# How one sample's query and key reach 128 partitions in a retention layer: GpSimd broadcasts, or DMA through a DRAM scratch

## The chip, the core and the metric

The kernel runs on one core of a Trainium2 chip. The core has TensorE (PE, with its weight loads listed apart as PEld), VectorE (DVE), ScalarE (ACT), GpSimd (POOL) and SyncE (SP), which here issues almost all DMAs; 16 DMA engines carry them. The metric is device time in microseconds. Before the change the median of three runs is 2573.97 us (2573.81 to 2577.06).

## The reference

The program is one inference step of a two-layer trunk in float32 with width 2048: a pooling mixer, an MLP, a retention layer, a second MLP, each with a residual. It serves 272 prompt tokens (16 of them meta tokens) and 8 samples of one token, so 280 columns go through every matrix. The change lies in the retention layer, in the part that serves the samples. For each of 8 heads and each of 8 samples a state of 256 x 512 values is updated and read:

```
s_new = gamma[h] * s + outer(k, v)          # k: 256 values, v: 512 values
o     = q @ s_new                            # q: 256 values, o: 512 values
y     = head_norm(o) * silu(g);  x += y @ w_out
```

The new states are outputs too. For the prompt the same head does the chunked form (scores with decay, times values, and one final state).

## The kernel before

**Weights.** All matrices come as 388 units of 1 MB in one fixed stream, `wst`. `load_unit` (L107) loads one into a `raw` tile (three buffers), `conv_unit` (L116) splits it into a high part `wh` on ACT (L127) and a low part `wl` on DVE (L129), in two halves; for the o units of heads 5 and 6, which are in `POOLED`, the second half of `wl` is made on POOL. `mm_acc` (L142) then does three products per weight block (48 matmuls a unit, all on L147). A unit is split two units ahead of its use.

**Heads.** For each head the units are four v, two k, two q, and then a tail: four g (the gate) mixed with the four o units (output projection) of the head before. Head 0 and head 6 have only g in their tails, and head 7 has its four g, then the o units of heads 5 and 6; its own o units come last. An o unit has four PSUM tiles instead of one, each added into `xT` by DVE (L432); there are four PSUM buffers for all units.

**Attention beside the units.** `attention` (L471) is a generator: after each unit one step of it is written into the program, so that its small matmuls and the samples' work lie between the units. With `schedule_with_timeline_sim=True` a scheduler sets the final order of each engine's instructions; each engine then runs its own list strictly in order, and waits by semaphores. `keep_in_program_order` holds some DMAs in the order written.

**Samples.** State and output lie with the 512 features of v on partitions (four blocks of 128), so q and k of a sample are needed as the same row on all 128 partitions. `sample_rows` (L487) puts the columns of four samples 32 columns apart into a zeroed tile `spaced`, transposes it by four 128 x 128 transposes (L492), and ACT copies the result to `rows` (L494): now q and k of a sample are a row on one partition. It is done twice per head. In `sample` (L523) GpSimd spreads that row over all partitions:

```
bc = rp.tile([P, 2 * DK], F32, tag="bc", name="bc", bufs=2)
nc.gpsimd.partition_broadcast(bc, rows[b // 4][32 * (b % 4):32 * (b % 4) + 1, :])
```

ACT makes k times v (`kv`, L532, four pieces), DVE updates the state (L534, two halves) and reduces it against q (L537, four pieces, into `bc` itself), and the state is stored (L539). States have three buffers: sample b + 3 is loaded (L479) when the store of sample b is done. POOL has other work in the layer: the rotation of k and q (L412, L413), sums for the head norm (L586, L587), the gates (L598, L601), and the `wl` halves named above.

Of the kernel before, what the change touches and what calls it, by code (L numbers as in the profile page):

```python
# [10 lines left out]
F32 = mybir.dt.float32  # L11
# [5 lines left out]
P = 128  # L17
# [3 lines left out]
NTOK = 272  # L21
NS = 8
C = NTOK + NS
CQ = C - NMETA
H = 8
DK = 256
# [4 lines left out]
EPS = 1e-6  # L31
# [49 lines left out]
def trunk_step(ctx: ExitStack, tc: tile.TileContext, wst, xT_d, xtok_d, spool_d, xc_d, xs_d, gains_d, gB_d, band_d, cs_d,  # L81
               dec_d, kvec_d, sret_d, y_d, upt_d, ups_d, rp_d, rs_d):
    nc = tc.nc
# [17 lines left out]
    ident = pers.tile([P, P], F32, name="ident")  # L101
    e0 = pers.tile([P, 1], F32, name="e0")

    state = {"load": 0, "conv": 0, "mm": 0}
# [45 lines left out]
    def mm_tile(n):  # L150
        return pmm.tile([P, 512], F32, tag="mm", name="mm")[:, :n]

# [1 line left out]
    def prep(n, gi, cols, split=True):  # L154
        w = cols.stop - cols.start
        x = xT[:, n, cols]
# [16 lines left out]
            nc.scalar.activation(out=x, in_=x, func=AF.Copy, scale=g)  # L173

    def rsqrt(a, s):
        """a ** -0.5 into the last of s, refined by one Newton step."""
        r, t, o = s
        nc.scalar.activation(out=r, in_=a, func=AF.Sqrt)
        nc.vector.reciprocal(r, r)
        nc.vector.tensor_tensor(out=t, in0=r, in1=r, op=ALU.mult)  # L180
        nc.vector.tensor_tensor(out=t, in0=t, in1=a, op=ALU.mult)
        nc.vector.scalar_tensor_tensor(out=t, in0=t, scalar=-3.0, in1=r, op0=ALU.add, op1=ALU.mult)
        nc.vector.tensor_scalar_mul(o, t, -0.5)

    def token_rstd(parts, w, mean):
        """1 / sqrt(mean + EPS) of each token (tokens on partitions), spread on a diagonal."""
        nj = 4 if w == C else 3
        nt = w // nj
        ps = pst.tile([P, 512], F32, tag="st", name="st")
        for j in range(nj):  # L190
            for i, a in enumerate(parts):
                nc.tensor.matmul(ps[:nt, j:j + 1], a[:, j * nt:(j + 1) * nt], mean, start=(i == 0),  # L192
                                 stop=(i == len(parts) - 1))
        s = tmp.tile([P, 4, 4], F32, tag="rs", name="rs")
        a, r, t, o = [s[:nt, i, :nj] for i in range(4)]
        nc.vector.tensor_scalar_add(a, ps[:nt, :nj], EPS)
        rsqrt(a, (r, t, o))
        dg = tmp.tile([P, C], F32, tag="dg", name="dg", bufs=1)
        dg3 = dg[:nt, :w].rearrange("p (j t) -> p j t", j=nj)
        nc.vector.tensor_tensor(out=dg3, in0=ident[:nt, :nt].unsqueeze(1).to_broadcast([nt, nj, nt]),  # L200
                                in1=o.unsqueeze(2).to_broadcast([nt, nj, nt]), op=ALU.mult)
        return dg[:nt, :w]
# [13 lines left out]
    ALL = slice(0, C)  # L216
    QC = slice(NMETA, C)

    # ================= pooling mixer =================
    with tc.tile_pool(name="pp", bufs=1) as pp, tc.tile_pool(name="pd", bufs=1) as pd:  # L220
        hw = D // 2
        xTf = xT.rearrange("p a b -> p (a b)")
# [20 lines left out]
        for j, (x, r, c0, c1) in enumerate(((xc, NC, 241, 272), (xa, P, 0, 128), (xb, P, 128, 241))):  # L243
            s = st[:r, j]
# [3 lines left out]
                                           scale=1.0, scalar=0.0, accum_out=s[:, 1:2])  # L248
# [22 lines left out]
        for f in range(KT):  # L271
            w = f // 4
            fs = slice(f * P, (f + 1) * P)
            ps = patt.tile([P, 512], F32, tag="att", name="dps")[:, :C]
# [4 lines left out]
            else:  # L279
                nc.tensor.matmul(ps[:, 241:272], xc[:NC, fs], band[:NC, w, 241:272], start=True, stop=True)  # L280
                nc.tensor.matmul(ps[:, 272:280], xs[:, (f - 12) * P:(f - 11) * P], band[:, w, 280:288], start=True,
                                 stop=True)
            g = gains[:, 0, f:f + 1]
# [7 lines left out]
        for g in range(4):  # L291
            parts = begin_unit("pool")
            for i in range(4):
                n = g * 4 + i
                ps = mm_tile(C)
# [4 lines left out]
        nc.sync.dma_start(out=ups_d[:, 14], in_=xc[:NS])  # L300
        nc.gpsimd.dma_start(out=upt_d, in_=u2[NC - 15:NC])

    # ================= squared-ReLU MLP =================
    def mlp(i, cols, next_gi, split):
        T = cols.stop - cols.start
        with tc.tile_pool(name=f"mlp{i}", bufs=1) as mp:
# [40 lines left out]

    mlp(0, ALL, 2, True)

    # ================= retention =================  # L350
    with tc.tile_pool(name="rp", bufs=1) as rp, tc.tile_pool(name="rs", bufs=3) as rsp:
        cs = rp.tile([P, 2, C], F32, name="cs")
        nc.sync.dma_start(out=cs, in_=cs_d)
        kvec = rp.tile([P, H, 3], F32, name="kvec")
        nc.sync.dma_start(out=kvec, in_=kvec_d)
        mean_m = rp.tile([P, P], F32, name="mean_m")
        nc.vector.memset(mean_m, 1.0 / DV)
        spaced = rp.tile([P, 4, P], F32, name="spaced")
        nc.gpsimd.memset(spaced, 0.0)
        rtok = rp.tile([P, 3], F32, name="rtok")  # L360
        cos, sin = cs[:, 0], cs[:, 1]

        def tail_copies(src, n):
            """The prompt's last 16 columns of src [P, n, .], six times over."""
            t = rp.tile([P, 4, 6, 16], F32, tag="tail", name="tail")[:, :n]
            nc.scalar.copy(out=t, in_=src[:, :, JT[2][0]:NTOK].unsqueeze(2).to_broadcast([P, n, 6, 16]))
            return t.rearrange("p n r t -> p n (r t)")
# [68 lines left out]
        def att_ps():  # L436
            return patt.tile([P, 512], F32, tag="att", name="att")

        # values: token-major, split for the state and centred over the head's features for the output
        def v_tokens(h, j):  # L440
            vT = cur["v"]
            if j == 0:
# [17 lines left out]
            nc.scalar.activation(out=vc[:nt, j], in_=vc[:nt, j], func=AF.Identity, bias=acc[:nt, 3 + j:4 + j])  # L460

        def split(hi, lo, ps, nr, scale, r0):
            """High and low part of ps * scale; of the stacked tail rows, rows r0 to r0 + 32 of hi take the low part."""
            rows = slice(0, nr)
            nc.scalar.activation(out=hi[rows], in_=ps[rows], func=AF.Copy, scale=scale)
            if nr < P:
                rows, lo = slice(r0, r0 + 32), hi
            nc.vector.scalar_tensor_tensor(out=lo[rows], in0=ps[rows], scalar=scale[rows],
                                           in1=hi[rows].bitcast(F32), op0=ALU.mult, op1=ALU.subtract)

        def attention(h, last):  # L471
            qT, kT, vs, (vh, vl, vc) = cur["q"], cur["k"], cur["vs"], cur["vtok"]
            dec = rp.tile([P, DC], F32, tag="dec", name=f"dec{h}")
            nc.sync.dma_start(out=dec, in_=dec_d[h])
            sts = {}

            def load_state(b):
                t = rsp.tile([P, 4, DK], F32, tag="sret", name=f"s{h}_{b}")
                tc.keep_in_program_order(nc.sync.dma_start(out=t, in_=sret_d[h, b]))  # L479
                sts[b] = t  # L480

            for b in range(3):
                load_state(b)
            # queries and keys of four samples as rows on partitions 0, 32, 64 and 96
            rows = []

            def sample_rows(g):  # L487
                nc.vector.tensor_copy(spaced[:, 0:2, 0:P:32], qT[:, :, CQ - NS + 4 * g:CQ - NS + 4 * g + 4])
                nc.vector.tensor_scalar_mul(spaced[:, 2:4, 0:P:32], kT[:, :, NTOK + 4 * g:NTOK + 4 * g + 4], 1.0 / 16)
                ps = att_ps()  # L490
                for i in range(4):
                    nc.tensor.transpose(ps[:, i * P:(i + 1) * P], spaced[:, i], ident)  # L492
                r = rp.tile([P, 2 * DK], F32, tag="rows", name="rows")
                nc.scalar.copy(out=r, in_=ps)  # L494
                rows.append(r)

            sample_rows(0)
            # keys: token-major, decayed to the end of the prompt
            kdh, kdl = [rp.tile([P, n, DK], F32R, tag=f"kd{n}", name=f"kd{n}_{h}") for n in (3, 2)]
            cols = token_cols(kT, 2)  # L500
            for j in range(3):
                if j != 1:
                    ps = att_ps()
# [2 lines left out]
                    nc.tensor.transpose(ps[:RT[j], off + i * P:off + (i + 1) * P], cols(i, j), ident)  # L506
                split(kdh[:, j], kdl[:, min(j, 1)], ps[:, off:off + DK], RT[j], kvec[:RT[j], h, j:j + 1], 32)
            yield True
            # scores
            ps = att_ps()  # L510
            pr = rp.tile([P, DC], F32, tag="pr", name="pr")
            off = 0
            for j, (t0, nt, q0, nq) in enumerate(JT):
                for i in range(2):
                    nc.tensor.matmul(ps[:nt, off:off + nq], kT[:, i, t0:t0 + nt], qT[:, i, q0:q0 + nq], start=(i == 0),
                                     stop=(i == 1))
# [6 lines left out]
            def sample(b):  # L523
                if b + 3 < NS:
                    load_state(b + 3)
                bc = rp.tile([P, 2 * DK], F32, tag="bc", name="bc", bufs=2)
                nc.gpsimd.partition_broadcast(bc, rows[b // 4][32 * (b % 4):32 * (b % 4) + 1, :])  # L527
                s = sts[b]
                for z in range(2):
                    kv = rp.tile([P, 2, DK], F32, tag="kv", name="kv", bufs=2)  # L530
                    for i in range(2):
                        nc.scalar.activation(out=kv[:, i, :], in_=bc[:, 256:512], func=AF.Copy,  # L532
                                             scale=vs[:, 2 * z + i, b:b + 1])
                    nc.vector.scalar_tensor_tensor(out=s[:, 2 * z:2 * z + 2], in0=s[:, 2 * z:2 * z + 2],  # L534
                                                   scalar=GAMMA[h], in1=kv, op0=ALU.mult, op1=ALU.add)
                for i in range(4):
                    nc.vector.tensor_tensor_reduce(out=bc[:, 256:512], in0=s[:, i, :], in1=bc[:, 0:256], op0=ALU.mult,  # L537
                                                   op1=ALU.add, scale=1.0, scalar=0.0, accum_out=OS[:, i, b:b + 1])
                nc.sync.dma_start(out=rs_d[h, b], in_=s)  # L539
# [26 lines left out]
                work = {1: (prompt_o, 0), 2: (prompt_o, 1), 3: (prompt_state, 0), 4: (prompt_state, 1)}  # L566
            for b in range(NS):
                sample(b)
                if b == 3:
                    sample_rows(1)  # L570
                if b in work:
                    f, a = work[b]
                    f(a)
                yield not (last and b == 0)
            # head norm
            ps = pst.tile([P, 512], F32, tag="st", name="om")
            om = rp.tile([P, NS], F32, tag="om", name="om")
            nc.vector.tensor_reduce(out=om, in_=OS.rearrange("p v b -> p b v"), op=ALU.add, axis=mybir.AxisListType.X)  # L578
# [176 lines left out]
```

## Time and profile before

| | |
|---|---|
| median of three runs | 2573.97 us |
| the profiled execution, first to last instruction (its span) | 2567.0 us |
| lying around the span (median less span) | 7.0 us |
| PE busy in the span | 2493.4 us (97%) |
| DVE, ACT, POOL busy | 59%, 45%, 18% |
| granted TensorE clock, mean | 0.981 of full speed |
| DMA | 493.07 MB, 192 GB/s mean |

The profile is read from the wait backwards. A row of waits names who waited, who released it last, how long and how often. "issue" as releaser says that the profile shows nothing that the engine waited for. A busy PE is not a PE at full speed: its clock is granted (1.0 is 2.4 GHz, 0.5 is 1.2 GHz), so the number of matmuls in a stretch must be read beside the busy time. In a timeline, starts count; ends of matmuls overlap the next.

### The profile page before, as it was taken

What the parts mean: (1) busy time and instruction counts of PE and PEld (TensorE: products, weight loads), DVE (VectorE), ACT (ScalarE), POOL (GpSimd) and SP (SyncE); (2) the same over time, 40 slices, a digit from 0 to 9 for tenths busy, and PEclk for the clock granted to TensorE, in tenths of its full rate; (3) what the DMA queues carried; (4) which work ended last, traced back from release to release, by engine and by line L of the source; (5) the groups of instructions that cost most, each with busy time, mean ns of one, the idle gap of its engine ahead of it and who ended that gap; (6) DMA issues with size and microseconds to landing.
All of it is one profiled execution on the core that took longest, in us unless ns stands there. A gap on an engine that the chain in (4) does not pass through costs nothing. (4 is left out here: it accounts for less than half of the span.)

```text
span 2567.0 us, 46873 instructions
## 1 busy us (share of the span) xinstructions
PE 2493.4 (97%) x19590; PEld 2470.3 (96%) x19590; DVE 1526.7 (59%) x2430; ACT 1158.3 (45%) x1660; POOL 466.3 (18%) x381
## 2 busy tenths in 40 slices
PE   8999999999999999999999999868999999999997
PEld 8999999999999998999999999857999999999997
DVE  7554554554555576777867767645654554554554
ACT  5433333343344465566655656524433333433443
POOL 4210210110122112112121122214210210210222
PEclk9999999999999998999999999978999999999999
DMA  6444454454444574766757566534555554554453
GB/s 235 167 171 174 179 177 168 166 179 165 172 171 169 196 257 179 277 217 231 265 204 286 201 253 242 190 131 156 175 186 182 181 181 181 181 181 181 181 181 116
DMA packets 81943, 493.07 MB, mean 192 GB/s; under 512 B 9216, under 2 KB 12288, under 8 KB 31608
## 3 DMA queue, kind: packets, MB, share of 16 engines
q1 hardware_dynamic: 81699, 489.95, 53.4%
q8 instruction: 153, 2.51, 0.4%
q14 instruction: 59, 0.48, 0.1%
q0 software_dynamic: 32, 0.12, 0.0%
HBM read 449.94 MB, written 41.02 MB: 191 GB/s over the span
## 5 line engine op out<-in xcount | busy, mean ns | idle before, releaser
L127 ACT CAST wh<-raw 128x1024 fp32r<-128x1024 f32 x776 | 799.8, 1050 | 1181.2 <-PE mm L147 644.3
L129 DVE TENSOR_TENSOR wl<-raw,wh 128x1024 fp32r<-128x1024 f32 x768 | 998.1, 1330 | 79.4 <-ACT wh L127 78.1
L147 PE MATMUL mm<-xh,wh 128*128 128x280 f32 (+1 forms) x3584 | 492.4, 290 | 2.4 <-DVE om L578 1.2
L147 PE MATMUL mm<-xh,wl 128*128 128x280 f32 (+1 forms) x3584 | 487.0, 288 | 0.0
L147 PE MATMUL mm<-xl,wh 128*128 128x280 f32 (+1 forms) x3584 | 484.8, 287 | 0.0
L147 PEld LDWEIGHTS mm<-xh,wh 128*128 128x128 f32 x3584 | 464.4, 189 | 5.3 <-ACT wh L127 2.7
L147 PEld LDWEIGHTS mm<-xh,wl 128*128 128x128 f32 x3584 | 463.1, 188 | 0.3
L147 PEld LDWEIGHTS mm<-xl,wh 128*128 128x128 f32 x3584 | 461.9, 188 | 0.0
L318 POOL TENSOR_TENSOR hf<-r 128x280 f32<-128x280 f32 (+1 forms) x128 | 185.2, 1448 | 1156.1 <-DVE r L314 1156.1
L344 DVE TENSOR_TENSOR xT<-mm,xT 128x280 f32<-128x280 f32 (+1 forms) x128 | 56.5, 441 | 400.9 <-PE mm L147 400.9
L147 PE MATMUL mm<-hh,wh 128*128 128x280 f32 (+1 forms) x2048 | 276.3, 287 | 0.0
L147 PE MATMUL mm<-hh,wl 128*128 128x280 f32 (+1 forms) x2048 | 276.2, 287 | 0.0
L147 PE MATMUL mm<-hl,wh 128*128 128x280 f32 (+1 forms) x2048 | 276.2, 287 | 0.0
L147 PEld LDWEIGHTS mm<-hh,wh 128*128 128x128 f32 x2048 | 263.8, 188 | 0.0
L147 PEld LDWEIGHTS mm<-hh,wl 128*128 128x128 f32 x2048 | 263.8, 188 | 0.0
L147 PEld LDWEIGHTS mm<-hl,wh 128*128 128x128 f32 x2048 | 263.7, 188 | 0.0
L314 DVE SCALAR_TENSOR_TENSOR r<-mm,rstd 128x280 f32<-128x280 f32 (+1 forms) x128 | 56.3, 441 | 303.3 <-PE mm L147 303.2
L532 ACT ACTIVATE kv<-bc,vs 128x256 f32<-128x256 f32 x256 | 110.3, 499 | 96.4 <-POOL bc L527 92.3
L147 PE MATMUL mm<-yh,wh 128*128 128x264 f32 x512 | 91.8, 303 | 40.4 <-DVE xT L432 28.9
L534 DVE SCALAR_TENSOR_TENSOR s<-s,kv 128x512 f32<-128x512 f32 x128 | 88.4, 697 | 70.5 <-ACT kv L532 65.8
L527 POOL PARTITION_BROADCAST bc<-rows x64 | 59.4, 960 | 333.8 <-DVE os L537 136.0
L147 PEld LDWEIGHTS mm<-yh,wh 128*128 128x128 f32 x512 | 76.9, 202 | 43.3 <-DVE xT L432 11.6
(173 smaller groups left out, 1685.3 us busy)
## 6 DMA issues: line engine op xcount, KB each, us to landing
raw<-in_wst SPq DMA_DIRECT2D x388, 1024.0 KB, 4.8
s<-in_sret SPq DMA_DIRECT2D x64, 512.0 KB, 6.1
out_rs<-s SPq DMA_DIRECT2D x64, 512.0 KB, 5.3
out_rp<-so SPq DMA_DIRECT2D x16, 256.0 KB, 2.8
xT<-in_xT SPq DMA_DIRECT2D x4, 560.0 KB, 15.1
dec<-in_dec SPq DMA_DIRECT2D x8, 208.0 KB, 2.8
out_y<-xT SPq DMA_DIRECT2D x2, 528.0 KB
xa<-in_xtok SPq DMA_DIRECT2D x1, 1024.0 KB, 7.3
```

What stands on the lines that cost most here:

```text
L127: nc.scalar.copy(out=wh, in_=src)
L129: eng.tensor_tensor(out=wl, in0=src, in1=wh.bitcast(F32), op=ALU.subtract)
L147: nc.tensor.matmul(ps, parts[s][z][:, kk, :], rhs[k][:, cols], start=(rhs is rhs_h and z + k == 0), stop=(rhs is rhs_l and k == n - 1))
L314: nc.vector.scalar_tensor_tensor(out=r[:, :T], in0=ps, scalar=0.0, in1=rstd[:, cols], op0=ALU.max, op1=ALU.mult)
L318: nc.gpsimd.tensor_tensor(out=hf[:, :T], in0=r[:, :T], in1=r[:, :T], op=ALU.mult)
L344: nc.vector.tensor_tensor(out=xT[:, n, cols], in0=ps, in1=xT[:, n, cols], op=ALU.add)
L527: nc.gpsimd.partition_broadcast(bc, rows[b // 4][32 * (b % 4):32 * (b % 4) + 1, :])
L532: nc.scalar.activation(out=kv[:, i, :], in_=bc[:, 256:512], func=AF.Copy, scale=vs[:, 2 * z + i, b:b + 1])
L534: nc.vector.scalar_tensor_tensor(out=s[:, 2 * z:2 * z + 2], in0=s[:, 2 * z:2 * z + 2], scalar=GAMMA[h], in1=kv, op0=ALU.mult, op1=ALU.add)
```

## The change

It touches the attention of the retention layer only. Per head, the queries and keys of all eight samples are copied together into one tile `qk` (128 x 32), one plain matmul with the identity turns it into 32 rows of 128, ACT copies these to SBUF, and one DMA writes them to a scratch `rd` in DRAM. Each sample's row of 512 values is then read back by one DMA with a step of 0 over partitions, which fills all 128 partitions of `bc`. The `bc` tile now has three buffers in the pool of the states, and its load is issued right behind the load of the same sample's state. The states of the first three samples are issued after the write of the scratch. `spaced`, `sample_rows` and all `partition_broadcast` are gone.

```diff
+    with tc.tile_pool(name="rp", bufs=1) as rp, tc.tile_pool(name="rs", bufs=3) as rsp, \
+            tc.tile_pool(name="rd", bufs=2, space=bass.MemoryType.DRAM) as rdp:
...
-        spaced = rp.tile([P, 4, P], F32, name="spaced")
-        nc.gpsimd.memset(spaced, 0.0)
...
             dec = rp.tile([P, DC], F32, tag="dec", name=f"dec{h}")
             nc.sync.dma_start(out=dec, in_=dec_d[h])
-            sts = {}
+            rd = rdp.tile([NS, 4, P], F32, tag="rd", name=f"rd{h}")
+            qk = rp.tile([P, 2, 2, NS], F32, tag="qk", name="qk")
+            nc.vector.tensor_copy(qk[:, 0], qT[:, :, CQ - NS:CQ])
+            nc.vector.tensor_scalar_mul(qk[:, 1], kT[:, :, NTOK:C], 1.0 / 16)
+            ps = att_ps()
+            nc.tensor.matmul(ps[:4 * NS, 0:P], qk.rearrange("p t i b -> p (t i b)"), ident, start=True, stop=True)
+            rows = rp.tile([4 * NS, P], F32, tag="rows", name="rows")
+            nc.scalar.copy(out=rows, in_=ps[:4 * NS, 0:P])
+            tc.keep_in_program_order(nc.sync.dma_start(out=rd.rearrange("b j f -> j b f"), in_=rows))
+            sts, bcs = {}, {}
 
             def load_state(b):
                 t = rsp.tile([P, 4, DK], F32, tag="sret", name=f"s{h}_{b}")
                 tc.keep_in_program_order(nc.sync.dma_start(out=t, in_=sret_d[h, b]))
                 sts[b] = t
+                t = rsp.tile([P, 2 * DK], F32, tag="bc", name=f"bc{h}_{b}")
+                row = rd[b:b + 1].rearrange("b j f -> b (j f)")
+                tc.keep_in_program_order(nc.sync.dma_start(out=t, in_=row.to_broadcast([P, 2 * DK])))
+                bcs[b] = t
 
             for b in range(3):
                 load_state(b)
-            rows = []
-            def sample_rows(g):
...
-            sample_rows(0)
...
             def sample(b):
                 if b + 3 < NS:
                     load_state(b + 3)
-                bc = rp.tile([P, 2 * DK], F32, tag="bc", name="bc", bufs=2)
-                nc.gpsimd.partition_broadcast(bc, rows[b // 4][32 * (b % 4):32 * (b % 4) + 1, :])
-                s = sts[b]
+                s, bc = sts[b], bcs[b]
...
                 sample(b)
-                if b == 3:
-                    sample_rows(1)
```

The scheduler's order changes with it. On POOL, in the tail of head 7, this stood before (`bc` is the broadcast of a sample, `oc` the gate's product, `wl` the low half of a weight unit; an ISA row without operands is an instruction of POOL's own between two kinds of work):

```order
L601 ISA
L601 TENSOR_TENSOR oc_17212<-oc_17212,ro 128x264 x4
L527 ISA
L527 ISA bc<-rows 128x512
L129 ISA
L129 TENSOR_TENSOR wl_1_18384<-raw_18097,wh_1_18383 128x1024
```

In the same place of the changed kernel (L412 rotates q, L596 is the gate's product) POOL has:

```order
L412 TENSOR_TENSOR qT_17923<-qT_17923,rpb 128x264
L596 TENSOR_TENSOR oc_17164<-oc_17164,ro 128x264 x4
L129 TENSOR_TENSOR wl_1_18327<-raw_18034,wh_1_18326 128x1024
L129 TENSOR_TENSOR wl_1_18413<-raw_18137,wh_1_18412 128x1024
L129 TENSOR_TENSOR wl_1_18496<-raw_18244,wh_1_18495 128x1024
L129 TENSOR_TENSOR wl_1_18575<-raw_18330,wh_1_18574 128x1024
L129 TENSOR_TENSOR wl_1_18654<-raw_18416,wh_1_18653 128x1024
```

Before, the last four rows come four times more, with other `wl` halves, until sample 7's broadcast is done. Now the broadcasts and all ISA rows between kinds are gone, and the `wl` halves stand one behind the other.

On SP, around the first samples of head 7 (`s` is a state, its first number the sample; `raw` a weight unit; `out_rs` a stored state), before:

```order
L479 DMA s_2_18157<-in_sret 128x1024
L113 DMA raw_17747<-in_wst 128x2048
L113 DMA raw_17852<-in_wst 128x2048
L113 DMA raw_17935<-in_wst 128x2048
L113 DMA raw_18011<-in_wst 128x2048
L113 DMA raw_18097<-in_wst 128x2048
L113 DMA raw_18194<-in_wst 128x2048
L539 DMA out_rs<-s_0_18153 128x1024
L539 DMA out_rs<-s_1_18155 128x1024
L479 DMA s_3_18259<-in_sret 128x1024
L113 DMA raw_18301<-in_wst 128x2048
L539 DMA out_rs<-s_2_18157 128x1024
```

and in the changed kernel (`rd` is the write of the scratch, `bc` the read of a sample's row):

```order
L113 DMA raw_18034<-in_wst 128x2048
L483 DMA rd_18090<-rows 4x8x128
L488 DMA s_0_18099<-in_sret 128x1024
L492 DMA bc_0_18101<-rd_18090 128x512
L488 DMA s_1_18103<-in_sret 128x1024
L492 DMA bc_1_18105<-rd_18090 128x512
L488 DMA s_2_18107<-in_sret 128x1024
L492 DMA bc_2_18109<-rd_18090 128x512
L113 DMA raw_18137<-in_wst 128x2048
L536 DMA out_rs<-s_0_18099 128x1024
L113 DMA raw_18244<-in_wst 128x2048
L536 DMA out_rs<-s_1_18103 128x1024
```

Before, the states of samples 0 to 2 are loaded six weight units ahead of the first store; now they stand directly ahead of it, behind the write of the scratch, each followed by its row.

On DVE, in head 4, this ends with the decayed scores `pr`, which the next small matmuls of PE read (L534 a state update, L537 a reduce, `kd` keys for the prompt's state); the two updates of sample 0 stand some rows ahead of these, before:

```order
L534 SCALAR_TENSOR_TENSOR s_1_14492<-s_1_14492,kv 128x512
L432 TENSOR_TENSOR xT<-mm,xT 128x264
L534 SCALAR_TENSOR_TENSOR s_1_14492<-s_1_14492,kv 128x512
L468 SCALAR_TENSOR_TENSOR kd_4_14506<-att,kvec,kd_4_14505 128x256
L537 ISA bc,os<-s_0_14490,bc 128x256
L537 ISA os 128x1
L518 TENSOR_TENSOR pr<-att,dec_14488 128x400
L519 TENSOR_TENSOR pr<-att,dec_14488 16x16
```

and in the changed kernel, with sample 0's updates among the rows (L531 is the state update, L534 the reduce, L517 and L518 make `pr`):

```order
L531 SCALAR_TENSOR_TENSOR s_0_14463<-s_0_14463,kv 128x512
L431 TENSOR_TENSOR xT<-mm,xT 128x264
L531 SCALAR_TENSOR_TENSOR s_0_14463<-s_0_14463,kv 128x512
L534 ISA bc_0_14465,os<-s_0_14463,bc_0_14465 128x256
L534 ISA os 128x1
L467 SCALAR_TENSOR_TENSOR kd_4_14476<-att,kvec,kd_4_14475 128x256
L517 TENSOR_TENSOR pr<-att,dec_14452 128x400
L518 TENSOR_TENSOR pr<-att,dec_14452 16x16
```

In both, work that PE reads later (`xT` sums, `wl`, `pr`) stands behind the first state update of sample 0; `pr` now comes after sample 0's updates instead of after sample 1's.

## Rows read from the trace of the kernel before

**Rows 1.** The page: span; each engine's busy us, share, instructions.
```profile
span 2567.0 us, 46873 instructions
...
PE 2493.4 (97%) x19590; PEld 2470.3 (96%) x19590; DVE 1526.7 (59%) x2430; ACT 1158.3 (45%) x1660; POOL 466.3 (18%) x381
```

**Rows 2.** Stretches: length; busy us (instructions) by engine; PEclk, DMA, GB/s.
```profile
980.07:1103.73 123.66, 116.83 (x865) 112.26 (x865) 85.53 (x182) 68.29 (x113) 30.71 (x33) 0.94 0.58 210
1103.73:1212.87 109.14, 109.14 (x856) 107.25 (x856) 81.10 (x170) 64.51 (x105) 21.50 (x22) 1.00 0.67 239
...
1643.28:1780.20 136.92, 92.41 (x606) 88.33 (x604) 63.48 (x151) 47.45 (x80) 37.80 (x28) 0.78 0.39 144
```

**Rows 3.** Waits of PE, 1640 to 1790 us: us, times, longest.
```profile
PE mm L147 <- DVE xT L432: 28.5, 3, 10.7
PE mm L147 <- DVE gs L422: 7.5, 1, 7.5
PE att L547 <- DVE pr L519: 6.8, 1, 6.8
```

**Rows 4.** Waits of all engines, 1640 to 1760 us.
```profile
ACT kv L532 <- POOL bc L527: 62.9, 6, 16.5
...
POOL bc L527 <- issue: 42.4, 5, 9.4
```

**Rows 5.** Timeline of POOL, head 7: start, us, instruction [idle before <- releaser].
```profile
1726.44 0.80 POOL L527 PARTITION_BROADCAST bc<-rows  x1 [9.36 <-issue]
1734.25 2.35 POOL L129 TENSOR_TENSOR wl<-raw,wh 128x1024 fp32r<-128x1024 f32 x1 [7.01 <-issue]
```

**Rows 6.** Line 527: op xcount: ns min/median/max, first, last start.
```profile
L527 POOL PARTITION_BROADCAST bc<-rows x64: 798/803/1917, 915.5 to 1745.5; - x64
...
L527 POOLq MODIFY_POOL_CONFIG  x28: 1/6/16, 909.8 to 1736.8; - x28
```

**Rows 7.** Timeline of PE in head 4, undisturbed: start, us, instruction.
```profile
1346.17 1.71 PE L515 MATMUL att<-qT,kT 128*128 128x256 f32 x12
1347.81 2.21 PE L147 MATMUL mm<-xh,wh 128*128 128x264 f32 x16
...
1353.73 2.36 PE L547 MATMUL att<-pr,vc 128*128 128x256 f32 x12
1356.02 0.76 PE L147 MATMUL mm<-yh,wh 128*128 128x264 f32 x4
...
1361.96 2.35 PE L547 MATMUL att<-pr,vc 128*128 128x256 f32 x12
...
1370.16 0.60 PE L492 MATMUL att<-ident,spaced 128*128 128x128 f32 x4
1370.52 0.72 PE L557 MATMUL att<-vh,kd 128*128 128x512 f32 x2
...
1372.24 0.65 PE L147 MATMUL mm<-yh,wh 128*128 128x264 f32 x4
```

**Rows 8.** Timeline of ACT in head 4, around the first broadcast.
```profile
1340.37 0.58 ACT L494 COPY rows<-att 128x512 f32<-128x512 f32 x1
...
1343.30 0.90 ACT L532 ACTIVATE kv<-bc,vs 128x256 f32<-128x256 f32 x2
```

**Rows 9.** The page: DMA issues: count, KB each, median us from issue to landing.
```profile
s<-in_sret SPq DMA_DIRECT2D x64, 512.0 KB, 6.1
out_rs<-s SPq DMA_DIRECT2D x64, 512.0 KB, 5.3
out_rp<-so SPq DMA_DIRECT2D x16, 256.0 KB, 2.8
```

**Rows 10.** DMA queue, 1342 to 1396 us: packets, MB, share.
```profile
q1 hardware_dynamic: 3496, 15.16, 78.8%
```

**Rows 11.** The page: state update on DVE: count | busy us, mean ns.
```profile
L534 DVE SCALAR_TENSOR_TENSOR s<-s,kv 128x512 f32<-128x512 f32 x128 | 88.4, 697 | 70.5 <-ACT kv L532 65.8
```

**Rows 12.** Reduce on DVE, tile bc: ns min/median/max.
```profile
L537 DVE CUSTOM_DVE_ANT_0 bc<-s,bc x256: 406/418/964, 918.9 to 1752.1; 128x256 f32<-128x256 f32 x128
```

More of the change, by code (lines that the diff above doesn't have):

```diff
@@ L348, in trunk_step @@
     mlp(0, ALL, 2, True)
-    with tc.tile_pool(name="rp", bufs=1) as rp, tc.tile_pool(name="rs", bufs=3) as rsp:
+    with tc.tile_pool(name="rp", bufs=1) as rp, tc.tile_pool(name="rs", bufs=3) as rsp, \
+            tc.tile_pool(name="rd", bufs=2, space=bass.MemoryType.DRAM) as rdp:
         cs = rp.tile([P, 2, C], F32, name="cs")
@@ L480, in load_state @@
                 sts[b] = t
+                t = rsp.tile([P, 2 * DK], F32, tag="bc", name=f"bc{h}_{b}")
+                row = rd[b:b + 1].rearrange("b j f -> b (j f)")
+                tc.keep_in_program_order(nc.sync.dma_start(out=t, in_=row.to_broadcast([P, 2 * DK])))
+                bcs[b] = t
             for b in range(3):
                 load_state(b)
-            rows = []
-            def sample_rows(g):
[L488 to L495, printed above, removed]
-            sample_rows(0)
             kdh, kdl = [rp.tile([P, n, DK], F32R, tag=f"kd{n}", name=f"kd{n}_{h}") for n in (3, 2)]
```

## The prediction

> **What bounds the kernel now.** The page first: PE is busy for 2493.4 of 2567.0 us [rows 1], so on the whole only PE's own work, or one of its few gaps, can move the time. POOL, which the change relieves, is busy for 18%, and it would be wrong to stop there. The gaps are found by stretches. I cut the retention layer at the first rotation of k in each head. The four heads 2 to 5 take 109.14 us each at a granted clock of 1.00 and PE never idles (one of the four stands in the rows). Head 1 has the same units and takes 123.66 us at 0.94. From the first transpose for the samples of head 7 to its own o units 136.92 us pass at 0.78 with 606 matmuls, where an undisturbed head does 856 in 109.14 [rows 2].
>
> Next, who PE waits for in head 7: DVE, with 28.5 us for xT sums, 7.5 for a gate product and 6.8 for the scores `pr` [rows 3]. But DVE has nothing heavy there. It stands in order behind state updates, and these wait for ACT's `kv`, which waited for POOL's broadcast, 62.9 us in six waits; POOL's broadcasts began after 42.4 us of "issue" [rows 4], time in which it waited for nothing that the profile shows. The timeline of POOL gives the cause: whenever it changes between a broadcast and a `wl` half it idles, 9.36 us ahead of a broadcast of 0.80, then 7.01 ahead of a `wl` half [rows 5]. 28 MODIFY_POOL_CONFIG stand on POOL's queue at the broadcast's line [rows 6]; each broadcast that follows other work pays such a gap, and in head 7 the two kinds alternate five times. In heads 2 to 5 POOL changes kind early and the gap falls where nobody waits.
>
> **What the change removes.** *Head 7.* POOL has one kind of work left, so the alternation goes. What PE's work there takes at full clock and without a wait is read from head 4 [rows 7]. A g unit takes 1353.73 - 1347.81 = 5.92 us and an o unit 1361.96 - 1356.02 = 5.94. In the stretch lie three g and eight o units: 11 x 5.93 = 65.2. The scores take 1347.81 - 1346.17 = 1.64, two groups of L547 at 2.29 take 4.6, two groups for the prompt's state at 1372.24 - 1370.52 = 1.72 take 3.4, the two groups of transposes at 0.36 take 0.7, and the sixteen or so small matmuls that remain, at the 0.09 of a transpose, some 1.5 by estimate. Sum 77.0; the loss is 136.9 - 77.0 = 59.9 us. About 44 of it is idle (136.92 less 92.41 busy); the rest is the granted clock, 0.78 in the mean, that follows the idle time, and it comes back with it.
>
> *Head 1.* 123.66 - 109.14 = 14.5 us, the same cause: in head 1 POOL must go from broadcasts to the gates' products of head 0 and back.
>
> *Transposes.* Two groups of four at 0.36 are 0.72 us a head on PE, which is the bound. In their place stands one plain matmul of 128 columns in float32. The trace has none of this shape. L515 does 832 columns of plain float32 in 1.64 us, so 128 cost 0.25; the least is a transpose, 0.09, the most all 0.72 again. I take 0.25, the row with the same kind of matmul: 0.47 saved a head, 3.8 in eight. The Trainium skill says in "TensorE: Matmul & The Clock Gate", section "Terms", that a transpose mode makes float32 four times as fast, which speaks against trading transposes for a plain matmul. By that the new one would cost 4 x 0.09 = 0.36 and the change would save 2.9 instead of 3.8, a time of 2501; the rows give a factor of 2.8, and they decide.
>
> *Off the path.* POOL loses 64 x 0.80 = 51 us of work and ACT one of two copies of 0.58 per head [rows 6, 8]; neither engine is waited for once the gaps are gone, so this is worth nothing.
>
> **What it adds.** 64 reads of 256 KB and 8 small writes, all issued by SP. In head 4 the old copy of the rows ends at 1340.95 and ACT's first `kv` begins at 1343.30 [rows 8], 2.35 us later. Now a write to the scratch must land, then a read. The trace has neither. Per DMA the nearest row is `out_rp`, 256 KB in 128 rows like the read: 2.8 us; the far rows are a state's store and load, 5.3 and 6.1 [rows 9]. So the first row is there after 5.6 us, or at the worst after 11.4. State 0, now issued right behind the write, lands 6.1 after it, when the first half of `kv` is made. I take 5.6, because the same shape moves as in `out_rp`. Then `kv` begins at 1346.6, its first half takes 0.90, and on DVE two updates at 0.70, one reduce at 0.42 [rows 11, 12] and four smaller instructions come to some 3.5 us: `pr` is ready at 1351.0. PE asks for it at 1353.73 [rows 7]; the delay is hidden with 2.7 us to spare. At the worst `pr` comes at 1356.8, and PE waits 3.0 us in each head. Behind the waiting update stand xT sums and `wl` halves as well; these are due later than `pr`. On SP, a weight unit stands behind the reads of samples 0 to 2. SP is held by the scratch write for 2.8 to 5.3 us, while the weights have three buffers, 17.8 us of PE's work: hidden. I charge 4 us in all, 0.5 a head, for landings above the median.
>
> The DMA engines have the room: in the sample stretch of head 4 they are busy for 78.8% of 54 us with 15.16 MB [rows 10], 356 GB/s while busy, so eight reads, 2.1 MB, take 5.9 us of the 11.4 that are free.
>
> **The sum.** The profiled span is 2567.0 us; the median of the runs shown is 2573.97, so 7.0 us lie around the span, and I leave these as they are. 2574.0 - 59.9 - 14.5 - 3.8 = 2495.8 is the floor; plus 4 it is 2500 us.
>
> **Rivals.**
> *DVE becomes the bound of head 7.* Its work there, 63.48 us [rows 2], would have to fit into 77.0 us, a share of 82%; the undisturbed heads show 81.10 of 109.14, 74%. For it: PE's tiles of an o unit come free only through DVE. Against it: a share of 74% never made PE wait. If 74% is what an in-order DVE can do, head 7 takes 63.48 / 0.743 = 85.4 us, 8.4 more than the floor: 2508 with the 4.
>
> *The two chained DMAs are slow.* If write and read together take over 8.3 us (5.6 and the 2.7 to spare), `pr` is late in every head. For it: landings of states of 5.3 and 6.1 under the same load. Against it: 16 KB and 256 KB are less than 512. At 11.4 us it costs 8 x 3.0 = 24: 2520.
>
> *The DMA engines fill up, and the kernel gets slower.* In each head eight reads of one DRAM row join a stretch that is already 78.8% busy. If a read costs the engines its whole landing of 2.8 us instead of 0.74, eight take 22.4 us, 11.0 more than is free; states and weights come later by that, PE has no slack of that size, and over eight heads it is 88 us: 2495.8 + 88 = 2584, slower than before. It decides from (11.4 + 78.2 / 8) / 8 = 2.65 us a read. For it: every read takes its 128 copies from the same 2 KB. Against it: the price of bytes in the same stretch.
>
> *The change doesn't do what it says.* POOL's idle time before `wl` halves is also called "issue"; if it isn't the change of kind that causes it, head 7 stays as it is and only the transposes gain: 2570, which is no change. Against it: 28 configurations stand in the trace at the broadcast's line [rows 6], and the changed order of POOL has none between its `wl` halves.
>
> **How the numbers follow.** The forecast, 2495 to 2506, has 0.58. DVE as the bound (2506 to 2512) has 0.12, the slow chain (2512 to 2535) 0.16, a remainder between 2535 and 2568 has 0.04, no effect 0.03, slower 0.07. Faster by over 0.2% (5.1 us, about what can be told from no change) is 0.58 + 0.12 + 0.16 + 0.04 = 0.90; within 0.2% 0.03; slower 0.07. The range goes from 2491, as the small matmuls in the 77.0 are an estimate, to 2535, and leaves out 0.14.
>
> **What would show it.** Right: no MODIFY_POOL_CONFIG between `wl` halves, head 7's stretch near 77 us and head 1 near 109, both at a clock of 1.00; heads 2 to 5 at about 108.7; the new matmul near 0.25; `rd` and `bc` landing within 2.8 us each. Wrong: PE waiting for `pr` in each head (slow chain), for xT in head 7 with a busy DVE (DVE bound), or heads 2 to 5 longer than 109.1 with DMA shares near 1 (engines full). A stretch of head 7 still above 100 us would overturn the reading of POOL's gaps.

## The result, and the profile after

The changed kernel takes 2500.51 us (median of 4 runs, 2498.72 to 2501.81) where the kernel before took 2573.89 beside it (4 runs): a ratio of 0.972, 95% interval 0.970 to 0.973. The profiled execution spans 2498.0 us and took 2499.76; its line numbers are those of the changed file.

The first lines of its page answer to [rows 1]; busy us, share of the span, instructions.

```profile
span 2498.0 us, 46727 instructions
...
PE 2470.1 (99%) x19542; PEld 2447.3 (98%) x19542; DVE 1519.3 (61%) x2414; ACT 1153.0 (46%) x1652; POOL 413.4 (17%) x316
```

PE is busy for 23 us less and idle for 46 us less. The stretches of [rows 2], cut at the same instructions: head 1, head 2, and head 7 from the samples' matmul to its own o units (length; busy us of PE, PEld, DVE, ACT and POOL; PEclk, DMA share, GB/s).

```profile
979.05:1091.57 112.52, 110.54 (x859) 107.45 (x859) 83.28 (x180) 67.56 (x112) 24.26 (x25) 1.00 0.69 250
1091.57:1200.34 108.77, 108.77 (x850) 106.56 (x850) 79.12 (x168) 63.80 (x104) 14.14 (x14) 1.00 0.72 259
1629.07:1711.43 82.36, 78.00 (x599) 74.77 (x598) 70.53 (x149) 47.19 (x79) 36.61 (x20) 1.00 0.79 284
```

Head 7 gives 136.92 - 82.36 = 54.6 us, head 1 11.1, and the six other heads 2.6 together (0.37 to 0.47 each); 0.7 lies elsewhere. That is 69.0, the whole difference of the two profiled spans; the medians differ by 73.4, since the profiled execution of the kernel before was one of its shorter ones. The granted clock in head 7 is back from 0.78 to 1.00. The waits of PE there, against the 43 us in [rows 3]:

```profile
PE mm L147 <- DVE xT L431: 3.9, 3, 2.0
```

No MODIFY_POOL_CONFIG is left on any line of the retention layer. The kernel before had 28 on the broadcasts' line [rows 6] and 28 more on the lines of the work that followed broadcasts (L129 and L586 10 each, L412 and L601 4 each). What became slower is the DMAs. From the page, in the columns of [rows 9]: count, KB each, median us to landing.

```profile
s<-in_sret SPq DMA_DIRECT2D x64, 512.0 KB, 6.3
out_rs<-s SPq DMA_DIRECT2D x64, 512.0 KB, 7.2
bc<-rd SPq DMA_DIRECT2D x64, 256.0 KB, 7.6
out_rp<-so SPq DMA_DIRECT2D x16, 256.0 KB, 7.4
```

The read of a row lands after 7.6 us in the median, not after 2.8, and `out_rp`, from which I took the 2.8, now needs 7.4 itself. But only 18 of the 64 reads have a recorded landing, and none of these is of samples 0 to 2, while the prediction's step is about sample 0. For the first read of head 4, SP's issues (first fence) and ACT's timeline (second) answer to [rows 8].

```profile
1327.64 0.60 SPq L483 DMA_DIRECT2D rd<-rows  x1
...
1329.60 0.33 SPq L492 DMA_DIRECT2D bc<-rd  x1
```

```profile
1327.36 0.25 ACT L482 COPY rows<-att 32x128 f32<-32x128 f32 x1
...
1334.40 1.71 ACT L529 ACTIVATE kv<-bc,vs 128x256 f32<-128x256 f32 x4 [3.05 <-DMA bc<-rd]
```

The first `kv` begins 6.8 us behind the copy, where I had 5.6: 2.0 us from the issue of the write to that of the read, and then at most 4.8 to the landing of the read. PE does not wait for `pr` in any head.

### The profile page after: what moved, and what is told of

Same layout as the page of the kernel before. It is cut to its first block, busy times and chain, and to the rows that moved or that the text cites. A ratio compares the mean times of both kernels' runs of the same rounds, so it can differ in the third digit from the quotient of the medians.

```text
span 2498.0 us, 46727 instructions
## 1 busy us (share of the span) xinstructions
PE 2470.1 (99%) x19542; PEld 2447.3 (98%) x19542; DVE 1519.3 (61%) x2414; ACT 1153.0 (46%) x1652; POOL 413.4 (17%) x316
## 4 chain that ended last, share of the span: by engine, by line
PE 94%; DVE 2%; POOL 1%; DMA 1%; ACT 1%; issue 1%; SPq 0%; DVEq 0%; POOLq 0%; ACTq 0%
PE mm L147 90%; PE att L544 1%; PE att L554 1%; DMA u<-in_gB 1%; DVE wl L129 0%; PE att L514 0%; DVE bc L534 0%; POOL oc L593 0%; PE att L455 0%; DVE s L531 0%; DVE xl L170 0%; DVE xT L431 0%; PE st L192 0%; DMA bc<-rd 0%; PE att L505 0%
## 5 line engine op out<-in xcount | busy, mean ns | idle before, releaser
L129 DVE TENSOR_TENSOR wl<-raw,wh 128x1024 fp32r<-128x1024 f32 x768 | 987.4, 1318 | 80.4 <-ACT wh L127 79.2
L534 DVE CUSTOM_DVE_ANT_0 bc<-s,bc 128x256 f32<-128x256 f32 x256 | 109.5, 440 | 1.7
L531 DVE SCALAR_TENSOR_TENSOR s<-s,kv 128x512 f32<-128x512 f32 x128 | 92.3, 729 | 23.3 <-ACT kv L529 22.6
L166 POOL TENSOR_TENSOR ssq<-ssq,sq 128x280 f32<-128x280 f32 (+1 forms) x56 | 70.9, 1266 | 172.7 <-ACT sq L164 172.2
L147 PE MATMUL mm<-yh,wh 128*128 128x264 f32 x512 | 86.0, 288 | 6.6 <-DVE xT L431 4.4
## 6 DMA issues: line engine op xcount, KB each, us to landing
xT<-in_xT SPq DMA_DIRECT2D x4, 560.0 KB, 15.2
```

The source lines that it names most:

```text
L129: eng.tensor_tensor(out=wl, in0=src, in1=wh.bitcast(F32), op=ALU.subtract)
L147: nc.tensor.matmul(ps, parts[s][z][:, kk, :], rhs[k][:, cols], start=(rhs is rhs_h and z + k == 0), stop=(rhs is rhs_l and k == n - 1))
L166: nc.gpsimd.tensor_tensor(out=ssq[:, cols], in0=ssq[:, cols], in1=sq[:, :w], op=ALU.add)
```

## The experiments

**The theory** is that of the prediction: each change of POOL between a broadcast and other work costs 7 to 9 us on POOL, and this made the losses of head 7 and head 1. The rivals: the transposes and the new order gained the time, or the broadcast as the carrier of the data did. Head 7 is timed as above in all of them.

**e1: the kernel before, without POOL's other work in head 7.**

```diff
-POOLED = frozenset(u for u, (k, h, _) in enumerate(ORDER)
-                   if (k, h) in {("o", H - 2), ("o", H - 3)})
+POOLED = frozenset()
```

> The kernel before, with its broadcasts on POOL, but all wl halves on DVE. My theory (POOL's change between kinds of work, 7 to 9.4 us each way, is what head 7 lost): of the ten changes in head 7 two round trips are left, so most of the 59.9 us goes; head 7 from 136.9 to 80 to 100 us, the whole 2514 to 2537 us; head 1 stays at 123.7. Rival (the gain came from the new order, the transposes or the data path): head 7 stays above 120 us and the whole above 2555.

2520.06 us (2519.33 to 2520.87), ratio to before 0.979 [0.978, 0.981]: nearly three quarters of the gain without any of the change's own edits. Head 1 stayed at 123.94; head 7's stretch and PE's only wait in it:

```profile
1643.91:1733.31 89.40, 81.48 (x606) 78.59 (x604) 69.88 (x160) 48.25 (x81) 21.63 (x20) 0.92 0.62 220
```

```profile
PE att L547 <- DVE pr L519: 7.5, 1, 7.5
```

So neither the transposes nor the data path made most of head 7's loss. But this run also takes the halves off POOL. The next puts the changes of kind back and leaves all else.

**e3: the changed kernel with broadcasts that nobody reads.**

```diff
                 nc.sync.dma_start(out=rs_d[h, b], in_=s)
+                un = rp.tile([P, 1], F32, tag="un", name="un")
+                nc.gpsimd.partition_broadcast(un, OS[0:1, 3, b:b + 1])
```

> The changed kernel, and per sample one more broadcast on POOL, of one element, whose result nobody reads; the data still come by DMA. If the change of kind on POOL is the cause, seven round trips of 7 + 8.5 us stand between the wl halves of head 7 (24 us): head 7 takes 110 to 140 us and the whole 2528 to 2570. Rival (the broadcast's data and its waits were the cause): no change, 2499 to 2505. On the time around the span: 7 us if it belongs to the presence of broadcasts, 1.8 us if it was chance.

2599.64 us (2598.13 to 2602.98), ratio 1.010 [1.009, 1.012]: slower than the kernel before. POOL's timeline in head 7:

```profile
1709.37 0.81 POOL L538 PARTITION_BROADCAST un<-os  x1 [9.70 <-issue]
1717.34 2.33 POOL L129 TENSOR_TENSOR wl<-raw,wh 128x1024 fp32r<-128x1024 f32 x1 [7.17 <-issue]
1728.77 0.30 POOL L538 PARTITION_BROADCAST un<-os  x1 [9.10 <-issue]
1736.17 2.33 POOL L129 TENSOR_TENSOR wl<-raw,wh 128x1024 fp32r<-128x1024 f32 x1 [7.10 <-issue]
```

A broadcast of one element that has no reader costs the gap of [rows 5] on either side. It reads what a reduce on DVE wrote and could have made POOL wait for that, but the idle time in these rows is "issue". PE's waits in head 7, and its length:

```profile
PE mm L147 <- POOL wl L129: 59.0, 6, 14.5
PE st L192 <- POOL osq L584: 13.4, 1, 13.4
```

```profile
1647.29:1811.36 164.07, 91.17 (x600) 87.22 (x599) 62.81 (x149) 47.36 (x79) 36.74 (x28) 0.77 0.42 142
```

This shows the cause for head 7. It does not test head 1: there POOL's broadcasts for the head's samples come only behind the gates' products, and the head takes what it takes in the changed kernel:

```profile
979.27:1091.79 112.52, 110.55 (x859) 107.46 (x859) 83.21 (x180) 67.35 (x112) 27.36 (x33) 1.00 0.70 250
```

That the same gaps made the 123.66 us of head 1 is read from the kernel before and not shown by a run. There the gates' products stood behind a broadcast, and PE's longest wait in the head (2.85 us for `yh`, until 1014.39) hung on them:

```profile
1004.16 1.48 POOL L527 PARTITION_BROADCAST bc<-rows  x2 [7.79 <-issue]
1013.16 3.23 POOL L601 TENSOR_TENSOR oc<-oc,ro 128x264 f32<-128x264 f32 x4 [7.52 <-issue]
```

My size for e3 was 30 us too small: I counted POOL's own time, not the halves and the last norm behind it, nor the 4 us that heads 2 to 5 each lost (112.7 to 114.4). The time around the span was 1.7 to 1.8 us in these runs, so broadcasts do not make it.

**e2: the changed kernel, all halves on DVE.** Head 7 still lay 5.4 us over the forecast, and DVE had gone from 63.48 to 70.53 us of busy time with fewer instructions. Its timeline (first fence) beside POOL's (second):

```profile
1664.12 0.68 DVE L531 SCALAR_TENSOR_TENSOR s<-s,kv 128x512 f32<-128x512 f32 x1
1664.72 2.62 DVE L534 CUSTOM_DVE_ANT_0 bc<-s,bc 128x256 f32<-128x256 f32 x1
...
1668.56 2.58 DVE L534 CUSTOM_DVE_ANT_0 bc<-s,bc 128x256 f32<-128x256 f32 x1
```

```profile
1664.46 2.59 POOL L129 TENSOR_TENSOR wl<-raw,wh 128x1024 fp32r<-128x1024 f32 x1 [5.54 <-ACT wh L127]
1667.95 2.90 POOL L129 TENSOR_TENSOR wl<-raw,wh 128x1024 fp32r<-128x1024 f32 x1 [0.90 <-ACT wh L127]
```

A reduce that takes 0.42 [rows 12] takes 2.6 when a half on POOL has begun just before it, and it ends 0.3 us behind that half. The edit is that of e1, made in the changed kernel.

> The changed kernel with all wl halves on DVE. Theory on what is left in head 7 (82.4 us against 77): DVE's instructions of 0.42 us stretch to 2.5 while POOL makes a half, so without these head 7 takes 77 to 79 us and the whole 2495 to 2497. Rival (DVE has too much work there): eight more halves at 1.13 us are 9 us more on DVE, head 7 takes 85 to 90 us and the whole 2504 to 2508.

2500.62 us (2497.16 to 2501.63): no gain. By the same two groups of head 7 in the changed kernel (first) and here (second; count | busy us, mean ns | idle before) the stretching is gone, and the added halves cost DVE a little less than it did (the sums stand in the last section):

```profile
L534 DVE CUSTOM_DVE_ANT_0 bc<-s,bc 128x256 f32<-128x256 f32 x32 | 19.4, 614 | 0.2
...
L531 DVE SCALAR_TENSOR_TENSOR s<-s,kv 128x512 f32<-128x512 f32 x16 | 16.5, 1052 | 2.1 <-ACT kv L529 2.1
```

```profile
L534 DVE CUSTOM_DVE_ANT_0 bc<-s,bc 128x256 f32<-128x256 f32 x32 | 13.0, 415 | 0.1
L531 DVE SCALAR_TENSOR_TENSOR s<-s,kv 128x512 f32<-128x512 f32 x16 | 10.9, 683 | 2.4 <-ACT kv L529 2.2
```

The stretch and the wait that took over:

```profile
1632.19:1712.38 80.19, 76.84 (x599) 74.34 (x598) 69.69 (x160) 48.27 (x80) 12.46 (x12) 0.99 0.81 292
```

```profile
PE mm L147 <- ACT yh L597: 3.4, 1, 3.4
```

PE ran its 76.84 us of other work without a gap, then waited for head 7's own norm, which POOL made in 7.0 us beside the gates. So head 7 gained 2.2 us. The profiled execution as a whole gained nothing: its head 1 took 115.56, and after the wait for the norm the clock was at 0.50 from 1711.0 to 1717.8.

**e4: one transpose for the identity matmul.**

```diff
-            nc.tensor.matmul(ps[:4 * NS, 0:P], qk.rearrange("p t i b -> p (t i b)"), ident, start=True, stop=True)
+            nc.tensor.transpose(ps[:4 * NS, 0:P], qk.rearrange("p t i b -> p (t i b)"), ident)
```

> The changed kernel with its identity matmul (0.34 us) made a transpose, one per head. By the row of a transpose, 0.09 us, 0.25 us less per head, 2.0 in all: 2498.5. Rival (one transpose of 32 columns of weights costs the same, or the gap is hidden by something else): 2500.5.

2501.67 us (2497.16 to 2504.07), no difference that the totals can tell. The heads can tell it: 2 to 5 take 108.36 or 108.37 us each, against 108.74 or 108.77 (head 4 of the changed kernel, then of this one):

```profile
1309.08:1417.85 108.77, 108.77 (x850) 106.56 (x850) 79.16 (x168) 63.91 (x104) 14.13 (x14) 1.00 0.72 259
```

```profile
1310.58:1418.95 108.37, 108.37 (x849) 106.48 (x849) 79.27 (x168) 63.61 (x104) 14.14 (x14) 1.00 0.72 260
```

So 0.4 us a head, where I had 0.25. In the profiled execution head 1 (115.58) and head 7 (83.91) took it back.

**What head 1 does.** PE waits once in the changed kernel's head 1, 1.78 us for `yh` at 1002.75, and the same wait stands in e2 to e6 and in the second run of the changed kernel (e10). The stretch 1000 to 1010 us in the first run and in e10:

```profile
1000.00:1010.00 10.00, 8.22 (x50) 6.72 (x49) 6.57 (x17) 6.47 (x17) 3.23 (x4) 1.00 0.91 290
```

```profile
1000.00:1010.00 10.00, 8.22 (x35) 6.39 (x34) 6.89 (x17) 6.59 (x17) 3.23 (x4) 0.71 0.86 267
```

After the same gap the clock stays at 2.4 GHz in one execution and falls to 1.2 for part of the stretch in another; head 1 then takes 115.5 in place of 112.5 us. In the profiles of e3 and e5 it held, in those of e2, e4, e6 and e10 it fell. Why it falls in one and not in the other stays open.

**e7: no wait in head 1.**

```diff
+    if h == 1:
+        return gs + os_
     if h == H - 2:
         return gs
```

> The changed kernel with head 1's units in another order: its four g units, then the four o units of head 0. The wait of 1.78 us for yh in head 1, and the clock that falls behind it in some executions (0.68 to 0.72 over the next 10 us), make head 1 112.5 or 115.6 us in place of 108.77. If that wait is the cause, head 1 takes 108.8 to 109.5 and the whole 2494 to 2497. Rival (the units' order moves the wait to a g unit or into head 2): no gain, 2499 to 2502.

2497.68 us (2496.1 to 2498.55), ratio 0.972 [0.970, 0.973]. That is the ratio of the changed kernel too, since the kernel before took 2569.23 beside this run, so the totals show no gain. Head 1 shows one: the wait is gone and the clock stays:

```profile
979.23:1089.43 110.20, 110.10 (x859) 107.60 (x859) 83.53 (x180) 67.44 (x112) 24.27 (x25) 1.00 0.71 255
```

PE is busy for all of these 110 us. So head 1 has more work than head 2: the norms of two heads fall into it (in the changed kernel's lines 4 matmuls of L206 and 12 of L192 in place of 2 and 6). Head 2 takes 108.77, so the head that I compared it with was 1.4 us too short.

**e5 and e9: a longer chain of DMAs.** Two more DRAM tiles stand between the rows and their reads:

```diff
-            tc.keep_in_program_order(nc.sync.dma_start(out=rd.rearrange("b j f -> j b f"), in_=rows))
+            tc.keep_in_program_order(nc.sync.dma_start(out=r0.rearrange("b j f -> j b f"), in_=rows))
+            tc.keep_in_program_order(nc.sync.dma_start(out=r1, in_=r0))
+            tc.keep_in_program_order(nc.sync.dma_start(out=rd, in_=r1))
```

> The changed kernel, whose rows pass two more DRAM tiles (16 KB each) before they are read. The prediction gave the chain of DMAs 2.5 to 2.7 us of slack before PE waits for the scores pr. Two hops more at 2.5 to 3.3 us each bring the first kv 5 to 6.6 us later. If the slack is what I read, PE waits 2.5 to 4 us in each of heads 2 to 6, these take 111 to 113 us in place of 108.77, and the whole 2515 to 2535 us. Rival (the chain of DMAs is hidden deeper): no wait for pr, 2499 to 2505.

2506.86 us (2504.77 to 2510.78). The chain became as long as meant, and heads 2 to 5 kept their 108.73 to 108.77. From head 4, by engine (ACT's `kv`, DVE's `pr`, PE's use of it); the copy of the rows ended at 1328.35:

```profile
1341.87 1.71 ACT L531 ACTIVATE kv<-bc,vs 128x256 f32<-128x256 f32 x4 [6.64 <-DMA bc<-rd]
```

```profile
1336.40 0.57 DVE L519 TENSOR_TENSOR pr<-att,dec 128x400 f32<-128x400 f32 x1
...
1341.39 2.38 PEld L546 LDWEIGHTS att<-pr,vc 128*128 128x128 f32 x12
```

The scheduler put `pr` ahead of the state updates, so that it no longer stood behind the chain, and no wait came. The profiled execution spans 5.0 us more than that of the changed kernel; head 7 alone takes 5.3 more (87.70). To judge my slack, e9 holds `pr` behind the updates of sample 0:

```diff
+                if b == 0:
+                    tc.keep_in_program_order(nc.vector.tensor_tensor(out=pr[:, 0:400], in0=sc[:, 0:400],
+                                                                     in1=dec[:, 0:400], op=ALU.mult))
```

> The kernel of e5 (two DRAM hops more, first kv 13.5 us behind the copy of the rows), with pr held on DVE behind the state updates of sample 0, where it stood in the changed kernel; in e5 it had moved ahead of them. If the slack of 2.5 us that I read is right for that order, pr is ready some 3.0 us behind the first kv and 3.5 us after PE asks: waits for pr of 3 to 5 us in heads 2 to 6, 112 to 115 us each, the whole 2524 to 2540. Rival (PE has other work it can do there): as e5, 108.77 each and 2505 to 2511.

2517.73 us (2513.51 to 2519.83). Now PE waits, but briefly (all heads):

```profile
PE att L549 <- DVE pr L535: 5.0, 7, 1.6
```

Heads 2 to 5 take 109.2 to 109.8, not 112 to 115; most of the rest of the loss lies in heads 0, 1 and 7 (86.1, 114.0 and 91.6). The mechanism is there. Its price was 0.7 us a wait where I had 3 to 5: the first `kv` came 12.3 us behind the copy and not 13.5, and the scheduler also put other matmuls ahead of PE's use of `pr`, which comes 15.2 us behind the copy here (1333.83 to 1349.06) and 13.2 in the changed kernel. With its own order kept in full, the chain's limit wasn't tried.

**e6: more reads of rows.**

```diff
                 tc.keep_in_program_order(nc.sync.dma_start(out=t, in_=row.to_broadcast([P, 2 * DK])))
+                if b > 2:
+                    un = rp.tile([P, 2 * DK], F32, tag="un", name="un")
+                    tc.keep_in_program_order(nc.sync.dma_start(out=un, in_=row.to_broadcast([P, 2 * DK])))
```

> The changed kernel, and samples 3 to 7 of each head read their row a second time, 256 KB each, into a tile that nobody reads. If a read costs the DMA engines its bytes (0.74 us by 356 GB/s), five more take 3.7 us of the 5.5 left per head and PE waits for nothing new: 2499 to 2506. Rival (a read of one DRAM row by all partitions costs its whole landing, 2.65 us or more): 13 us per head, 8 more than is free, some 60 us: 2560.

2506.79 us (2505.76 to 2507.54). Heads 2 to 5 keep their 108.74 to 108.77, and PE never waits in them with five more reads of 256 KB per head. So the engines have the room that the bytes give, and the rival of full DMA engines falls. The profiled execution spans 7.8 us more than that of the changed kernel, and 7.7 of these lie in head 1 (115.67, the clock) and head 7 (86.83). So head 7 has less slack than the others; which late landing starts it there stays open.

**e8, e10, e11: the edits together.** e8 is the changed kernel with the edits of e2, e4 and e7, and the last head's two sums of squares on DVE:

```diff
-            nc.gpsimd.tensor_tensor(out=sq[:, 0:2], in0=sq[:, 0:2], in1=sq[:, 2:4], op=ALU.add)
-            nc.gpsimd.tensor_tensor(out=sq[:, 0], in0=sq[:, 0], in1=sq[:, 1], op=ALU.add)
+            eng = nc.vector if last else nc.gpsimd
+            eng.tensor_tensor(out=sq[:, 0:2], in0=sq[:, 0:2], in1=sq[:, 2:4], op=ALU.add)
+            eng.tensor_tensor(out=sq[:, 0], in0=sq[:, 0], in1=sq[:, 1], op=ALU.add)
```

> The changed kernel with the order of e7, the transpose of e4, all wl halves on DVE as in e2, and the two sums of squares of the last head on DVE in place of POOL, where they took 7.0 us beside the gates. By the rows: 3.0 from the transposes (0.38 per head), 3.7 to 6.8 from head 1, and 5.4 from head 7 (82.4 to 77) if the wait for yh of 3.4 us goes too: 2485 to 2489. Rival (each of these gives its time back elsewhere, as e2 and e4 did): 2497 to 2501.

2490.99 us (2490.74 to 2492.9), ratio 0.969 [0.968, 0.971], 2 us above what I expected. Since the kernel before took 2569.23 on that chip, it ran again beside the changed kernel.

> The changed kernel itself once more, on the same chip as e11, as its measure: ratio to before 0.970 to 0.973.

> The kernel of e8 once more beside e10. If its gain is real, 6 to 10 us less than e10 (the rows gave 3.0 in the heads, 2.7 or more in head 1, 2.4 in head 7). Rival: e8's gain came from the chip it ran on, within 3 us of e10.

The changed kernel took 2501.2 us (2499.34 to 2502.5), its ratio 0.9725 [0.9712, 0.9738]; the combined one 2489.74 (2489.42 to 2492.04), 0.9684 [0.9671, 0.9697]. It beats both kernels, the changed one by 11.5 us, where I had 6 to 10. Its heads 1, 2 and 7:

```profile
978.30:1088.13 109.83, 109.71 (x858) 107.53 (x858) 83.19 (x180) 67.34 (x112) 24.27 (x24) 1.00 0.71 256
1088.13:1196.51 108.38, 108.38 (x849) 106.49 (x849) 79.39 (x168) 63.71 (x104) 14.13 (x15) 1.00 0.71 260
1623.61:1701.64 78.03, 76.53 (x600) 74.39 (x597) 68.81 (x161) 47.61 (x80) 8.00 (x10) 1.00 0.84 300
```

Against e10 (115.54, 108.77 and 81.63) that is 5.7 in head 1, 0.4 in each plain head and 3.6 in head 7. PE is idle for 1.5 us in the last.

## Why the prediction was right, and where it was wrong

The time was right, and so was the cause: for head 7 by experiment (e1, e3), for head 1 by its rows alone. That the sum came out within 1 us was luck. The gains were forecast 9.2 us too large (78.2 for 69.0); against them stood 4.8 us too many around the span and 4 us charged for landings that made PE wait nowhere.

*Outside the span.* "7.0 us around the span" was wrong: I took the span of one execution from the median of others. In the 23 runs of the kernel before that stood beside the experiments, the time is 2.2 or 2.3 us over the span, with spans from 2566.1 to 2572.7; so the profiled one took about 2569. Against it the terms (78.2 gained, 4 lost) give 2495, and 2499.76 came. One should make the sum in spans when the profiled run's own time is not known.

*Head 7.* Right in mechanism (e1, e3), with 54.6 gained for 59.9. The forecast of PE's full-speed work, 77.0, holds to 0.5 us (76.84 in e2, 76.53 in e11). What the step left out is the cost of a half on POOL to DVE, which the old waits had covered, and the norm of head 7, which POOL makes late. Without the halves on POOL head 7 gets 2.2 us back (e2), and with all edits together, the norm's sums off POOL among them, 3.6 (e11 against e10). It is the rival "DVE becomes the bound" in part, at 82.4 instead of 85.4 us and by another mechanism: DVE was not short of time by its own work. The Trainium skill has the rule, in "SBUF — State Buffer", section "Who interferes with whom": a DVE instruction with two SBUF inputs contends with a GpSimd instruction that reads SBUF, over a shared pair of ports that it calls an exclusive lock. The trace agrees (0.42 against 2.6 us, ending 0.3 us behind POOL's).

*Head 1.* 11.1 gained for 14.5. One wait of PE stayed, with 2.3 us behind it (112.52 against 110.20 in e7), and the head's own work is 1.4 us more than that of head 2.

*Transposes.* 3.8 forecast; 2.6 was measured in the six heads where nothing else changed, 0.43 each, so 3.4 for eight. The trace shows 0.34 us from the start of the new matmul, two instructions, to that of the next (1326.30 to 1326.64, head 4), not 0.25. The rule that I weighed from the Trainium skill ("TensorE: Matmul & The Clock Gate", section "Terms") gave 0.36 for it by estimate and was nearer. Against one transpose, e4's heads say 0.4 for what it costs more; that its place on PE says only 0.23 more (0.34 to 0.11) stays unexplained.

*The chain of DMAs.* Both landings together were 1.2 us too short (6.8 for 5.6). The reads of later samples, which land after 7.6, were not in that step. I had read 2.8 from a store that now lands after 7.4 itself. The 4 us charged for it were not spent: PE waited for `pr` in no head. How much of the slack of 2.7 us was real isn't known: it was read from one order, and no run (e5, e9) kept that order.

*DMA room, and what POOL and ACT were relieved of:* right; worth nothing on the path, and e6 shows more room still.

## What to carry to other kernels

An engine that is busy for 18% can cost over 50 us (e1 won back 53), if each change between two kinds of its work costs 7 to 9 us and somebody waits for both: look at its idle time in front of cheap instructions. When such a wait goes, ask what the waiting covered; here it was the exclusion between two engines and a late norm. A slack read from one order is no bound where a scheduler will plan the order anew.

## What the runs showed of the hardware

- POOL's gap does not shrink with the size of the broadcast or for want of a reader. In head 7 it is 8.2 to 9.8 us ahead of a one-element broadcast and 7.0 to 7.2 on the way back (e3), against 7.5 to 9.4 and 6.8 to 8.6 with broadcasts of a whole row (before). Two broadcasts in a row take 1.48 us with no gap between them (before, 1706.13).
- A half on POOL takes 2.33 us alone (e3), and a 0.42 us reduce on DVE that begins behind it takes 2.6 us. With all halves on DVE, its reduces, updates and halves in head 7 come to 53.5 us (13.0 + 10.9 + 29.6, 24 halves); with eight of them on POOL to 54.3 (19.4 + 16.5 + 18.4, 15 halves in the stretch).
- One gap of 1.78 us on PE cost head 1 2.3 us or 5.3 (112.52 or 115.54 against 110.20), by whether the granted clock fell behind it. The changed kernel's four runs differ by 3.1 us, which is of that size.
